# Two transformer blocks in one program: the residual x stored by features instead of by tokens

## Chip, cores, metric

One core of one Trainium2 chip. The number compared is the device time of one execution in microseconds (us); a lower one is better. Three executions of the kernel before took 1293.08, 1286.48 and 1292.35 us, a median of 1292.35 us.

## The reference

Input is x with 256 tokens of 1024 features, two memories of 256 tokens (`mem`, `mem_2`) and all weights, everything in fp32. Two blocks follow one another. Cut to the lines that matter here:

```python
# block 1, layer 0 (retention) and layer 1 (differential attention)
memn = rms_norm(mem, mem_norm_w)
for layer in range(2):
    u = rms_norm(x, attn_norm_w[layer]) @ w_in[layer]
    o_main = ...            # retention, or differential attention with q, k normed per head
    o_mem = memory_attention(rms_norm(qc), ...memn @ w_mem_kv[layer]...)
    x = x + concat([o_main, o_mem]) @ w_out[layer]
    gu = rms_norm(x, ffn_norm_w[layer]) @ w_gate_up[layer]
    x = x + (silu(gu[..., :FFN_DIM]) * gu[..., FFN_DIM:]) @ w_down[layer]
# block 2
proj = rmsnorm(x, norm_mix_g) @ w_in_2
merged = sigmoid(gate_a) * y_gdn + sigmoid(gate_b) * y_gla     # two chunked recurrences
x = x + merged @ w_out_2
m = rmsnorm(mem_2, norm_mem_g)                                  # keys and values of cross attention
x = x + cross_attention(rmsnorm(x, norm_xattn_g), m) @ xattn_wo
x = x + square(relu(rmsnorm(x, norm_mlp_g) @ mlp_w1)) @ mlp_w2
return rmsnorm(x, norm_final_g)
```

`rms_norm(x, w)` is x divided by the root of the mean of its squares over the 1024 features (plus 1e-6), times w.

## The kernel before, in words

**Products in three parts.** Every weight product splits both operands into a high and a low part in fp32r and adds hi*hi, hi*lo and lo*hi in PSUM. Weights stream through `unit` (L261): one unit is two row blocks of 128 by up to 512 columns. Its steps are a load by SP's queue into `raw` (3 buffers), a cast to `hi` by ACT (L277) and a subtraction to `lo` by DVE (L185; every 8th unit by POOL). `hi` and `lo` have 4 buffers each. There are three ways to multiply with a unit:

- `proj` (L290): the activations are stationary, the weights move 512 columns. 12 matmuls a unit, two accumulators, and the result has a token on each partition.
- `proj_T` (L311): the weights are stationary, the activations move 256 columns.
- `proj_T2` (L338): the weights are stationary. High and low part of the activations lie side by side (`both`), so one matmul moves 512 columns for hi times both parts, and one of 256 adds lo times hi. 16 matmuls a unit, four accumulators of [128, 2, 256] whose two halves must be added afterwards, and the result has a feature on each partition.

**The residual.** x is two tiles of 128 tokens by 1024 features (`setup`, L367), loaded in `setup_rest` (L385). Each product that is added to it (`w_out`, `w_down`, `w_out_2`, `xattn_wo`, `mlp_w2`) goes through `out_proj` (L510): `proj` for the first 512 columns, an addition into x (`add_x`, L502), `proj` for the other 512, and another. The next layer wants x by features: `x_T2` (L636) transposes it with 4 PE transposes for each pair of features and splits the result into `H` tiles. `_Lazy` makes these splits when they are first asked for, so those of the first half of x are asked for while the second half's product runs (L514).

**Norms.** The products of a layer start with unnormalized x times the norm's gain. The factor of each token comes from `stats` (L245): four ACT squares with an accumulator, POOL's `rsqrt` (L200), and it is applied later. For the two memories `mem_stats` (L400) loads their rows for the same purpose, while `scaled_T` (L391) loads them transposed, in four loads of 512 KB into tiles of tag 'V', and splits them into `Z` tiles. The mixer multiplies x by the factor before it transposes (L774).

**Buffers and order.** `BUFS` (L144) sets how many buffers a tag has:

```python
BUFS = {'T': 14, 'G': 6, 'L': 22, 'H': 4, 'Z': 12, 'B': 4, 'V': 3}
```

A tile gets the buffer that was given out longest ago, and waits until that is read for the last time. 'V' serves the loads of `scaled_T` and the scratch of squares. The order of instructions on each engine is made by the scheduler of the tile framework from its own estimates when the program is built; on the chip each engine then works its list in order. `later` (L202) additionally holds an instruction behind the `lo` of a unit some units on.

**The start of the diff layer** (L645) comes right after ffn0's down product. PE runs two products of four units (`proj` at L648 and L752), then `scores(0, ...)` transposes the normalized result of the first, the `Z<-acc,tiny` tiles of L677. Between, DVE and ACT split the transposed mem_2 (L650), and `head_rms` (L406) computes the factors: square, reduction, POOL's `rsqrt` on 128x8.

## Time and profile before

| what | value |
| --- | --- |
| median of 3 runs | 1292.35 us (1286.48 to 1293.08) |
| the profiled execution | 1287.81 us, its span 1286.1 us, so 1.7 us lie around the span |
| PE busy | 1250.5 us, 97% of the span |
| DVE, ACT, POOL busy | 828.1, 678.8, 180.9 us (64%, 53%, 14%) |
| DMA | 215.72 MB, 168 GB/s on average |

The profiled execution is 4.5 us below the median. PE is busy nearly throughout, so two things move the time: what PE has to do, and the 36 us (1286.1 less 1250.5) in which it waits. Other engines matter where PE waits for them.

### The profile page before, as it was taken

How to read it: one execution, taken by the hardware profiler on the slowest of the kernel's cores; microseconds unless marked ns; L12 is line 12 of the kernel's file. 1: busy time of each engine (PE TensorE's matmuls, PEld its weight loads, DVE VectorE, ACT ScalarE, POOL GpSimd, SP SyncE). 2: the span in 40 equal slices, each digit the busy share in tenths (PEclk: the TensorE clock that was granted, in tenths of full speed). 3: DMA queues.
4: the chain of work that ended last, by engine and by line, in shares of the span. 5: the costliest groups of instructions: out<-in, count | busy, mean ns of one | idle time of the engine just before them, and what ended most of it. 6: DMA issues, size and time to landing. Idle time of an engine off the chain costs nothing.

```text
span 1286.1 us, 19034 instructions
## 1 busy us (share of the span) xinstructions
PE 1250.5 (97%) x7160; PEld 1071.6 (83%) x7160; DVE 828.1 (64%) x1299; ACT 678.8 (53%) x1088; POOL 180.9 (14%) x115
## 2 busy tenths in 40 slices
PE   8999999999999999999998999999999999999997
PEld 8787888888778888888878998867788897888886
DVE  6576677755876667674467787486635665788542
ACT  5655656545664565554467573343344444565442
POOL 0122110010420110100101021221111000001011
PEclk9999999999999999999999999999999999999999
DMA  8826566656644256665653545224365552565653
GB/s 297 279 87 203 176 196 185 196 195 192 187 131 148 83 164 201 192 190 189 195 176 115 181 121 170 84 70 142 112 194 175 172 177 86 166 207 178 201 190 107
DMA packets 147005, 215.72 MB, mean 168 GB/s; under 512 B 15456, under 2 KB 71904, under 8 KB 146912
## 3 DMA queue, kind: packets, MB, share of 16 engines
q1 hardware_dynamic: 146336, 213.27, 53.3%
q8 instruction: 56, 0.92, 0.3%
q10 hardware_dynamic: 432, 0.70, 0.2%
q0 software_dynamic: 144, 0.52, 0.1%
q14 instruction: 37, 0.30, 0.1%
HBM read 213.02 MB, written 1.44 MB: 167 GB/s over the span
## 4 chain that ended last, share of the span: by engine, by line
PE 84%; DVE 6%; DMA 3%; ACT 3%; issue 2%; POOL 1%; SPq 1%; POOLq 0%; ACTq 0%; DVEq 0%
PE acc L207 74%; PE ps L207 7%; PE ps L210 2%; DVE lo L185 2%; ACT hi L277 1%; DVE T L185 1%; DMA raw<-in_w_in_dram 1%; POOL tiny L200 1%; DVE L L185 1%; ACT T L195 1%; SPq L1053 0%; DMA constants<-in_small_dram 0%; DVE B L185 0%; DMA B<-in_mem_dram 0%; SPq L1029 0%
## 5 line engine op out<-in xcount | busy, mean ns | idle before, releaser
L277 ACT CAST hi<-raw 128x1024 fp32r<-128x1024 f32 (+1 forms) x393 | 407.1, 1039 | 413.3 <-PE acc L207 326.7
L185 DVE TENSOR_TENSOR lo<-raw,hi 128x1024 fp32r<-128x1024 f32 (+1 forms) x341 | 412.5, 1214 | 316.5 <-ACT hi L277 312.3
L207 PE MATMUL acc<-H,hi 128*128 128x512 f32 (+1 forms) x1696 | 470.5, 347 | 1.8 <-ACT hi L277 1.7
L207 PE MATMUL acc<-H,lo 128*128 128x256 f32 x1328 | 372.2, 281 | 0.0
L207 PEld LDWEIGHTS acc<-H,hi 128*128 128x128 f32 x1696 | 296.3, 190 | 43.7 <-ACT hi L277 2.5
L207 PEld LDWEIGHTS acc<-H,lo 128*128 128x128 f32 x1328 | 252.4, 190 | 1.8 <-issue 0.8
L185 POOL TENSOR_TENSOR lo<-raw,hi 128x1024 fp32r<-128x1024 f32 (+1 forms) x52 | 124.2, 2389 | 796.2 <-ACT hi L277 618.8
L207 PE MATMUL acc<-hi,H 128*128 128x512 f32 (+1 forms) x672 | 212.4, 392 | 1.2 <-ACT H L195 0.6
L207 PE MATMUL acc<-hi,Z 128*128 128x512 f32 x544 | 171.4, 391 | 0.0
L207 PE MATMUL acc<-hi,L 128*128 128x512 f32 x512 | 160.2, 390 | 0.0
L207 PEld LDWEIGHTS acc<-hi,H 128*128 128x128 f32 x672 | 125.3, 189 | 27.9 <-issue 1.8
L207 PE MATMUL acc<-lo,H 128*128 128x512 f32 (+1 forms) x336 | 131.6, 392 | 0.8 <-DVE lo L185 0.8
L207 PEld LDWEIGHTS acc<-hi,Z 128*128 128x128 f32 x544 | 102.1, 188 | 20.9
L207 PEld LDWEIGHTS acc<-hi,L 128*128 128x128 f32 x512 | 96.1, 188 | 19.8
L207 PE MATMUL acc<-lo,Z 128*128 128x512 f32 x272 | 106.0, 390 | 0.0
L207 PE MATMUL acc<-lo,L 128*128 128x512 f32 x256 | 99.7, 390 | 0.0
L207 PEld LDWEIGHTS acc<-lo,H 128*128 128x128 f32 x336 | 63.6, 189 | 14.6 <-DVE lo L185 1.7
L200 POOL TENSOR_TENSOR tiny<-tiny,constants 128x2 f32<-128x2 f32 (+4 forms) x41 | 41.4, 1012 | 238.6 <-DVE tiny L189 190.2
L207 PEld LDWEIGHTS acc<-lo,Z 128*128 128x128 f32 x272 | 51.1, 188 | 10.2
L207 PEld LDWEIGHTS acc<-lo,L 128*128 128x128 f32 x256 | 48.1, 188 | 9.8
L357 ACT COPY T<-acc 128x256 f32<-128x256 f32 x120 | 43.8, 369 | 12.8 <-PE acc L207 9.3
L185 DVE TENSOR_TENSOR T<-acc,T 128x256 f32<-128x256 f32 x120 | 44.9, 416 | 2.1 <-ACT T L357 2.1
(218 smaller groups left out, 1109.3 us busy)
## 6 DMA issues: line engine op xcount, KB each, us to landing
raw<-in_w_in_dram SPq DMA_DIRECT2D x91, 512.0 KB, 3.7
raw<-in_w_gate_up_dram SPq DMA_DIRECT2D x176, 256.0 KB, 3.4
raw<-in_mlp_w_dram SPq DMA_DIRECT2D x64, 512.0 KB, 4.3
raw<-in_w_down_dram SPq DMA_DIRECT2D x44, 512.0 KB, 4.5
raw<-in_w_out_dram SPq DMA_DIRECT2D x24, 512.0 KB, 4.3
raw<-in_w_in_dram SPq DMA_DIRECT2D x42, 256.0 KB, 3.9
raw<-in_w_mem_kv_dram SPq DMA_DIRECT2D x8, 512.0 KB, 3.9
raw<-in_xattn_wk_dram SPq DMA_DIRECT2D x8, 512.0 KB, 3.8
```

The costliest lines, as they stand in the source:

```text
L185: return (eng or self.nc.vector).tensor_tensor(out=out, in0=a, in1=b, op=op)
L195: self.nc.scalar.activation(out, in_, f, scale=scale, bias=bias, **k)
L200: self.nc.gpsimd.tensor_tensor(out=out, in0=in_, in1=self.c('mhalf')[:, :n], op=ALU.pow)
L207: self.nc.tensor.matmul(out, lhsT, rhs, start=start, stop=stop, skip_group_check=True)
L210: self.nc.tensor.transpose(out, in_, self.ident[:in_.shape[0], :in_.shape[0]])
L277: nc.scalar.copy(hi[:, k, :W], raw[:, k, :W])
L357: self.nc.scalar.copy(out[:, a, :], accs[a][:, 1, :])
```

## The change

x lives in four tiles of [128, 2, 256] by features. They are loaded from the transposed input directly (`first_T`), and neither x nor the memories are loaded by rows any more: six loads of 512 KB are gone. The four products `w_out` (both layers), `w_down` (both), `w_out_2` and `xattn_wo`, 76 units in all, go through `proj_T2`, and `add_x` adds both halves of each accumulator into x, in ffn after a product with the row R of factors. `x_T2` splits x without a transpose. `stats` squares x on ACT, adds the squares on DVE into a 'G' tile, and gets the mean with two matmuls with a column of 1/1024. For the memories the squares are taken of the transposed tiles in `scaled_T`, so that loads, squares and the sum of the products in `add_x` share the three 'V' buffers. `mlp_w2` keeps `proj`; `rows` transposes x back for it with 16 transposes. The constants' first 16 columns are loaded ahead of the others. `split` makes one tile a feature block, and 'H' has 8 buffers.

```diff
-    BUFS = {'T': 14, 'G': 6, 'L': 22, 'H': 4, 'Z': 12, 'B': 4, 'V': 3}
+    BUFS = {'T': 14, 'G': 6, 'L': 22, 'H': 8, 'Z': 12, 'B': 4, 'V': 3}
...
+    def squares(self, sums, x):
+        if not sums:
+            sums.append(self.t('G', F32, (P, 2, S)))
+            self.act(sums[0], x, AF.Square)
+        else:
+            j = self.t('V', F32, (P, 2, S))
+            self.act(j, x, AF.Square)
+            self.tt(sums[0], sums[0], j, ALU.add)
...
+    def stats(self, sums=None):
+        if sums is None:
+            sums = []
+            for p in range(4):
+                self.squares(sums, self.x[p])
+        ps = self.psum(tag='sm')
+        v = sums[0][:, 0, :]
+        self.tt(v, v, sums[0][:, 1, :], ALU.add)
+        for t in range(2):
+            self.mm(ps[:, t:t + 1], v[:, t * P:(t + 1) * P], self.mean)
         ms = self.tiny(2)
...
+        self.ts(ms, ps[:, :2], EPS, ALU.add)
...
     def setup(self):
...
-        self.x = [self.cp.tile([P, D], F32, name=f"x{t}") for t in range(2)]
+        self.x = [self.cp.tile([P, 2, S], F32, name=f"x{p}") for p in range(4)]
...
-        nc.scalar.dma_start(out=self.const[:, :w1], in_=a['small'][:, :w1])
+        nc.scalar.dma_start(out=self.const[:, :w0], in_=a['small'][:, :w0])
+        nc.sync.dma_start(out=self.x[0], in_=a['xT'][:, 0:2, :])
+        nc.scalar.dma_start(out=self.const[:, w0:w1], in_=a['small'][:, w0:w1])
...
-    def scaled_T(self, src, gname, tag):
+    def scaled_T(self, src, gname, tag, sums):
         def pair(p):
             raw = self.t('V', F32, (P, 2, S))
             self.nc.sync.dma_start(out=raw, in_=src[:, 2 * p:2 * p + 2, :])
-            return self.split(raw, tag, [self.col(gname, 2 * p + a) for a in range(2)])
+            out = self.split(raw, tag, [self.col(gname, 2 * p + a) for a in range(2)])
+            self.squares(sums, raw)
+            return out
...
-    def mem_stats(self, ap):
-        m = [self.t('B', F32, (P, D)) for _ in range(2)]
-        for t in range(2):
-            self.nc.sync.dma_start(out=m[t], in_=ap[t * P:(t + 1) * P, :])
-        return self.stats(m)
...
     def add_x(self, accs, c, scale=None):
...
+        for f, acc in enumerate(accs):
+            x = self.x[2 * c + f // 2][:, f % 2, :]
+            if scale is None or isinstance(scale, float):
+                for h in range(2):
+                    if scale is None:
+                        self.tt(x, acc[:, h, :], x, ALU.add)
+                    else:
+                        self.stt(x, acc[:, h, :], scale, x, ALU.mult, ALU.add)
             else:
...
+                e = self.t('V')[:, :S]
+                self.nc.scalar.copy(e, acc[:, 1, :])
+                self.tt(e, acc[:, 0, :], e, ALU.add)
+                self.tt(e, e, scale)
+                self.tt(x, x, e, ALU.add)
...
-        self.add_x(self.proj(hT, w, [(0, 512)], order), 0, scale)
+        self.add_x(self.proj_T2(hT, w, [(0, 512)], order, None, only), 0, scale)
...
+    def x_T2(self, gname, off=0, R=None):
+        def pair(p):
+            cols = [self.col(gname, off + 2 * p + a) for a in range(2)]
+            if R is None:
+                return self.split(self.x[p], 'H', cols)
+            n = self.t('V', F32, (P, 2, S))
+            for a in range(2):
+                self.stt(n[:, a, :], self.x[p][:, a, :], cols[a], R)
+            return self.split(n, 'H')
...
     def diff_layer(self):
...
-        ms, r = self.stats(self.x)
-        mT2 = self.mT2 = self.scaled_T(self.a['mem_2T'], 'mem2', 'Z')
+        ms, r = self.stats()
+        self.m2sums = []
+        mT2 = self.mT2 = self.scaled_T(self.a['mem_2T'], 'mem2', 'Z', self.m2sums)
         mT2[7]
```

**What moves on the engines.** The lists that follow are the instructions of one engine in their order in the program; numbers after a name tell tiles apart.

DVE at the start of the diff layer, before: `Z_3208` and `Z_3216` are parts of mem_2, `lo_3297` and `lo_3316` the last two units of the second product, `Z_3242` is the first normalized tile, for which PE's transposes wait.

```order
312 L192 SCALAR_TENSOR_TENSOR Z_3208<-V_3205,constants,Z_3207 128x256 x2
313 L192 SCALAR_TENSOR_TENSOR Z_3216<-V_3213,constants,Z_3215 128x256 x2
314 L411 TENSOR_REDUCE tiny_3237<-V_3235 128x8
315 L189 TENSOR_SCALAR tiny_3237<-tiny_3237,tiny_3221 128x8
316 L185 TENSOR_TENSOR lo_3297<-raw_3293,hi_3296 128x1024
317 L411 TENSOR_REDUCE tiny_3246<-V_3244 128x8
318 L185 TENSOR_TENSOR lo_3316<-raw_3312,hi_3315 128x1024
319 L185 TENSOR_TENSOR Z_3242<-acc_3077,tiny_3240 128x512
320 L189 TENSOR_SCALAR tiny_3246<-tiny_3246,tiny_3221 128x8
321 L185 TENSOR_TENSOR lo_3441<-raw_3437,hi_3440 128x1024
```

DVE there, after: `V_3397` and `V_3408` are the last two loads of mem_2, `V_3405` and `V_3416` their squares, `lo_3514` the last unit of the second product, `lo_3639` to `lo_3677` units of the third, `Z_3440` the first normalized tile.

```order
381 L192 SCALAR_TENSOR_TENSOR Z_3402<-V_3397,constants,Z_3402 128x256
382 L185 TENSOR_TENSOR G_3384<-G_3384,V_3405 128x512
383 L185 TENSOR_TENSOR lo_3639<-raw_3635,hi_3638 128x1024
384 L185 TENSOR_TENSOR lo_3658<-raw_3654,hi_3657 128x1024
385 L192 SCALAR_TENSOR_TENSOR Z_3410<-V_3408,constants,Z_3410 128x256
386 L192 SCALAR_TENSOR_TENSOR Z_3413<-V_3408,constants,Z_3413 128x256
387 L185 TENSOR_TENSOR G_3384<-G_3384,V_3416 128x512
388 L432 TENSOR_REDUCE tiny_3435<-V_3433 128x8
389 L185 TENSOR_TENSOR lo_3677<-raw_3673,hi_3676 128x1024
390 L189 TENSOR_SCALAR tiny_3435<-tiny_3435,tiny_3419 128x8
391 L185 TENSOR_TENSOR G_3384<-G_3384 128x256
392 L185 TENSOR_TENSOR Z_3440<-acc_3267,tiny_3438 128x512
```

Between the last `lo` of the second product and the first normalized tile there stood nothing; now there stand the splits of the last two loads of mem_2, the additions of their squares and three units.

SP's queue there, before: the loads of mem_2 among those of the weights, with what each waits for.

```order
189 L395 DMA V_3189<-in_mem_2T_dram 128x512 [waits Activation_49]
190 L395 DMA V_3197<-in_mem_2T_dram 128x512 [waits Activation_49]
191 L395 DMA V_3205<-in_mem_2T_dram 128x512 [waits DMAHW0_49,Activation_49]
192 L271 DMA raw_3293<-in_w_in_dram 128x2x256 [waits DMAHW1_49,DVE_49]
193 L271 DMA raw_3293<-in_w_in_dram 128x2x256 [waits DMAHW2_49]
194 L271 DMA raw_3312<-in_w_in_dram 128x2x256 [waits DMAHW3_49,DVE_49]
195 L395 DMA V_3213<-in_mem_2T_dram 128x512 [waits DMAHW6_49,DMAHW4_49,DVE_49]
```

SP's queue there, after:

```order
184 L281 DMA raw_3491<-in_w_in_dram 128x2x256 [waits DMAHW4_49,DMAHW5_49,DVE_49,Activation_49]
185 L412 DMA V_3376<-in_mem_2T_dram 128x512 [waits DVE_49,Activation_49]
186 L281 DMA raw_3491<-in_w_in_dram 128x2x256
187 L412 DMA V_3386<-in_mem_2T_dram 128x512 [waits DVE_49]
188 L281 DMA raw_3510<-in_w_in_dram 128x2x256 [waits DMAHW1_49,DMAHW6_49,DMAHW0_49,Pool_49]
189 L281 DMA raw_3510<-in_w_in_dram 128x2x256 [waits DMAHW7_49]
190 L281 DMA raw_3635<-in_w_in_dram 128x2x256 x2
191 L412 DMA V_3397<-in_mem_2T_dram 128x512 [waits DMAHW2_49,DMAHW3_49,DVE_49,Activation_49]
192 L281 DMA raw_3654<-in_w_in_dram 128x2x256 [waits DMAHW4_49,DVE_49]
193 L281 DMA raw_3654<-in_w_in_dram 128x2x256
194 L412 DMA V_3408<-in_mem_2T_dram 128x512 [waits DMAHW5_49,DVE_49]
```

Three of the four loads stood together and waited for ACT; now each of the four waits for DVE, and loads of weights stand behind each.

DVE between the two halves of layer 0's `w_out`, before (`lo_1314` and `lo_1332` are the second half's first two units):

```order
130 L189 TENSOR_SCALAR L_1193<-ps_1188,qkw 128x512
131 L185 TENSOR_TENSOR lo_1314<-raw_1311,hi_1313 128x1024
132 L185 TENSOR_TENSOR lo_1332<-raw_1329,hi_1331 128x1024
133 L185 TENSOR_TENSOR x_75<-acc_1195,x_75 128x512
134 L185 TENSOR_TENSOR x_76<-acc_1196,x_76 128x512
135 L185 TENSOR_TENSOR lo_1375<-raw_1371,hi_1374 128x1024
```

DVE there, after (`lo_1313` and `lo_1347` are the second half's first two units, `acc_1206` to `acc_1209` the first half's result):

```order
147 L192 SCALAR_TENSOR_TENSOR H_1332<-x_75,constants,H_1332 128x256
148 L185 TENSOR_TENSOR lo_1313<-raw_1310,hi_1312 128x1024
149 L185 TENSOR_TENSOR T_1179<-acc_1106,tiny_1195 128x256
150 L185 TENSOR_TENSOR x_76<-acc_1208,x_76 128x256
151 L185 TENSOR_TENSOR x_76<-acc_1209,x_76 128x256
152 L189 TENSOR_SCALAR L_1204<-ps_1199,qkw 128x512
153 L185 TENSOR_TENSOR x_76<-acc_1208,x_76 128x256
154 L185 TENSOR_TENSOR x_76<-acc_1209,x_76 128x256
155 L192 SCALAR_TENSOR_TENSOR H_1335<-x_75,constants,H_1335 128x256
156 L192 SCALAR_TENSOR_TENSOR H_1338<-x_76,constants,H_1338 128x256
157 L192 SCALAR_TENSOR_TENSOR H_1341<-x_76,constants,H_1341 128x256
158 L185 TENSOR_TENSOR lo_1347<-raw_1344,hi_1346 128x1024
```

Ahead of the second unit's `lo` there stood no addition into x; now the additions and splits of the first half do.

## Rows read from the trace of the kernel before

**Rows 1.** The page: span, and busy time of each engine with its share and instructions.

```profile
span 1286.1 us, 19034 instructions
...
PE 1250.5 (97%) x7160; PEld 1071.6 (83%) x7160; DVE 828.1 (64%) x1299; ACT 678.8 (53%) x1088; POOL 180.9 (14%) x115
```

**Rows 2.** Timeline of PE in ffn0's up projection: a `proj_T2` stretch. Columns: start us, us.

```profile
198.73 0.39 PE L207 MATMUL acc<-H,hi 128*128 128x512 f32 x1
...
204.27 0.39 PE L207 MATMUL acc<-H,hi 128*128 128x512 f32 x1
```

**Rows 3.** Timeline of PE in ffn0's down projection: a `proj` stretch.

```profile
299.83 0.62 PE L207 MATMUL acc<-hi,Z 128*128 128x512 f32 x2
...
302.55 0.62 PE L207 MATMUL acc<-hi,Z 128*128 128x512 f32 x2
```

**Rows 4.** Groups of PE by shape, then the timeline around one group of eight transposes of x.

```profile
L210 PE MATMUL ps<-constants,x 128*128 128x128 f32 x80 | 10.4, 272 | 0.0
...
L210 PE MATMUL ps<-constants,B 128*128 128x128 f32 x16 | 2.2, 279 | 0.7 <-DVE B L189 0.7
...
138.21 1.03 PE L210 MATMUL ps<-constants,x 128*128 128x128 f32 x8
139.00 0.48 PE L207 MATMUL acc<-H,hi 128*128 128x512 f32 x1
139.32 0.28 PE L207 MATMUL acc<-H,lo 128*128 128x256 f32 x1
```

**Rows 5.** Timeline of PE in the retention layer: 32 small matmuls.

```profile
77.55 3.68 PE L207 MATMUL ps<-L,T 128*128 128x64 f32 x32
```

**Rows 6.** Timeline of ACT and PE at the start; the landing of tile V there (us).

```profile
5.62 0.91 ACT L195 ACTIVATE H<-V,constants 128x256 fp32r<-128x256 f32 x2 [2.88 <-DMA constants<-in_small_dram]
...
7.08 1.22 PE L207 MATMUL acc<-H,hi 128*128 128x256 f32 x4 [1.75 <-ACT hi L277]
...
DMA to landing us min/median/max: 4.5/4.9/6.4
```

**Rows 7.** Busy time by stretch, a column per engine: PE first; then clock, DMA share, GB/s.

```profile
40.00:50.00 10.00, 8.91 (x39) 6.77 (x38) 5.55 (x10) 7.74 (x13) 2.39 (x1) 1.00 0.90 302
```

**Rows 8.** Groups by shape (busy us, mean ns | idle us before): DVE, ACT, POOL.

```profile
L185 DVE TENSOR_TENSOR lo<-raw,hi 128x1024 fp32r<-128x1024 f32 x332 | 406.5, 1228 | 312.7 <-ACT hi L277 308.6 <-PE acc L207 3.6
L185 DVE TENSOR_TENSOR T<-acc,T 128x256 f32<-128x256 f32 x120 | 44.9, 416 | 2.1 <-ACT T L357 2.1
L192 DVE SCALAR_TENSOR_TENSOR H<-ps,constants,H 128x256 fp32r<-128x256 f32 x56 | 24.4, 478 | 3.3 <-ACT H L195 2.9
...
L195 ACT ACTIVATE V<-x 128x512 f32<-128x512 f32 x32 | 19.9, 622 | 12.5 <-DVE x L192 11.0 <-DVE lo L185 0.8 <-DMA x<-in_x_dram 0.8
...
L200 POOL TENSOR_TENSOR tiny<-tiny,constants 128x8 f32<-128x8 f32 x6 | 11.8, 1973 | 16.4 <-DVE tiny L189 16.4
```

**Rows 9.** Timeline of DVE at the start of the diff layer.

```profile
316.76 1.40 DVE L192 SCALAR_TENSOR_TENSOR x<-acc,tiny,x 128x512 f32<-128x512 f32 x2
...
328.75 1.93 DVE L192 SCALAR_TENSOR_TENSOR Z<-V,constants,Z 128x256 fp32r<-128x256 f32 x2 [1.66 <-ACT Z L195]
...
334.36 0.69 DVE L185 TENSOR_TENSOR Z<-acc,tiny 128x512 f32<-128x512 f32 x1
```

**Rows 10.** Timeline of PE there.

```profile
340.15 1.03 PE L210 MATMUL ps<-constants,Z 128*128 128x128 f32 x8
...
343.00 1.57 PE L207 MATMUL ps<-T,T 64*128 64x128 f32 x12 [0.45 <-ACT T L690]
...
353.04 0.59 PE L210 MATMUL ps<-constants,T 128*128 128x128 f32 x2 [1.86 <-DVE T L192]
```

**Rows 11.** Timeline of SP's queue there, and the landing of tile V (us).

```profile
318.95 1.55 SPq L395 DMA_DIRECT2D V<-in_mem_2T_dram  x3
...
323.96 0.34 SPq L395 DMA_DIRECT2D V<-in_mem_2T_dram  x1
...
DMA to landing us min/median/max: 3.5/4.4/4.6
```

More of the change, by code (lines that the diff above doesn't have):

```diff
@@ L328, in proj_T, with acc2, proj_T2 @@
         return accs
-    def acc2(self):
+    def acc2(self, only=None):
         self.n += 1
         self.n2 += 1
-        if self.n2 % 3:
+        if only or self.n2 % 3:
             return self.pa.tile([P, 2, S], F32, tag="acc", name=f"acc{self.n}")
         return self.ps.tile([P, 2, S], F32, tag="pg", name=f"acc{self.n}", bufs=2)
-    def proj_T2(self, hT, w, cols):
+    def proj_T2(self, hT, w, cols, order=None, meanwhile=None, only=None):
         W = sum(b for _, b in cols)
-        accs = [self.acc2() for _ in range(W // P)]
+        accs = [self.acc2(only) for _ in range(W // P)]
         n = len(hT)
-        for k0 in range(0, n, 2):
-            hT[k0]
-            hi, lo = self.unit(w, k0, 2, cols)
+        order = order or list(range(n))
+        for i in range(0, n, 2):
+            hT[order[i]]
+            if i == 2 and meanwhile:
+                meanwhile()
+            hi, lo = self.unit(w, order[i], 2, cols)
             for f in range(W // P):
@@ L1393, in run @@
         else:
-            for t in range(2):
-                self.nc.sync.dma_start(out=self.a['out'][0, t * P:(t + 1) * P, :], in_=self.x[t])
+            for t, x in enumerate(self.rows()):
+                self.nc.sync.dma_start(out=self.a['out'][0, t * P:(t + 1) * P, :], in_=x)
 @with_exitstack
```

155 lines of the change are left out of this document (75 added, 80 removed).

## The prediction

> **What bounds the kernel now.** I read the totals first: PE is busy 1250.5 us of a span of 1286.1, so only 35.6 us are waits of PE; DVE has 64% and ACT 53% [rows 1]. Work taken from DVE or ACT is therefore worth nothing by itself, work on PE counts in full, and every step that makes PE wait counts in full too. Next I read PE's rhythm in the two kinds of stretches whose exchange is the change: the start of equal matmuls in `proj_T2` [rows 2] and in `proj` [rows 3], and the price of eight transposes between two products [rows 4]. Then I looked for the places at which PE waits or nearly waits and which the change touches: the start [rows 6], the stretch full of DMA behind it [rows 7], and the start of the diff layer, where four views belong together: DVE's list [rows 9], PE's [rows 10], SP's queue and the landing of its loads [rows 11], and the durations of single operations [rows 8]. The sums are made against the profiled execution's 1287.8 us; the median of the runs, 1292.35 us, stands 4.5 above it, and I carry the difference over to the median.
>
> **PE's work: -2.7 us.** Transposes: 96 are removed (80 with x as input, 16 with the mixer's B) and 16 of `rows` come, so 80 fewer. Eight took 138.21 to 139.00, 0.79 us, and the next matmul was followed after 0.32 us in place of the 0.23 that others take, so 0.88 us for eight, 0.11 each [rows 4]. 80 x 0.11 = -8.8 us; without the delay behind them it would be -7.9. Products: 16 pairs of `proj_T2` took 198.73 to 204.27, so a unit of 8 pairs takes 2.77 us [rows 2]; a unit of `proj` takes 299.83 to 302.55, 2.72 us [rows 3]. 76 units x 0.05 = +3.8 us. The means: 18 matmuls of one column and two more for a row. The nearest row is 32 small ones in 3.68 us, 0.115 each [rows 5], so 20 x 0.115 = +2.3; they may fall where PE waits anyway, so 0 is the other end. I take the full price, since PE hardly waits. Sum -8.8 + 3.8 + 2.3 = -2.7.
>
> The Trainium skill ("TensorE: Matmul & The Clock Gate", section Back-to-back issue gap) gives an isolated gap of N/2.4 + 2.5 ns, 215.8 ns for 512 columns and 109.2 for 256. By it a unit of 16 matmuls would take 2.60 us and one of 12 would take 2.59, and 76 units would cost 0.8 us in place of 3.8; the rows disagree with both absolute numbers, and the trace decides.
>
> **The start: -1.** ACT's first split waited 2.88 us for the constants, at 5.62, and PE's first real matmul came at 7.08 [rows 6]. Now 16 columns come first. But that split also needs the load of x, which takes 4.5 to 6.4 us to land, 4.9 in the middle, so the load becomes the limit almost at once. A gain between 0 and 2.5; I take 1.
>
> **Fewer loads: -0.3.** Six loads of 512 KB, 3 MB, go, most of them in a stretch where DMA is at 0.90. There PE loses 10.00 - 8.91 = 1.1 us in ten [rows 7], which is the most that can come back there; part of that wait belongs to steps of ACT. I take 0.3.
>
> **Half boundary of layer 0's `w_out`: +1.** The additions into x now stand ahead of the `lo` of the second half's second unit. Behind the end of the first half DVE has about two additions of 128x256 at 0.42, one 128x512 operation at about 0.7, three splits at 0.48 and the `lo` of 1.23 [rows 8], together 4.2 us; PE has the first unit, 2.77, and a pair of the next, 0.35 [rows 2]. So PE waits 1.1 us. If ACT's casts come late it is 2; if the additions begin inside the last unit, as their accumulators end one after the other, 0. I take 1. At the other boundaries the same additions stand behind two prepared units, 5.4 us, against 12 operations of 0.42 and a split, 5.5: I put 0.5 on all of these together (0 to 2).
>
> **The start of the diff layer: +8.** This is the term that decides. Call T the end of ffn0's down product, 316.7 in the trace [rows 9]. Before, the four loads of mem_2 left SP at T+2 (three) and T+7 [rows 11], DVE had the last split of them at T+14 and the first normalized tile at T+18.4, done before PE came to the transposes at T+23.4 [rows 9, 10]. So PE waited there for nothing, and soon after for 0.45 and 1.86 us [rows 10].
>
> After, PE arrives earlier: 8 units of 2.72, T+21.8. But the three 'V' buffers now hold scratch of the additions, three squares of x, four loads and three squares of mem_2. The chain, with durations of rows 8 and pitches slightly below them: 12 additions and products of x (0.33 to 0.42 each), two splits, the `lo` that stands ahead, and the first addition of squares bring DVE to about T+8; only then is a buffer free and the first load leaves. The second leaves after the next addition, T+10, and lands 4.4 us later [rows 11], at T+14.4. Its two casts (1.0) and square (0.62), then DVE's splits, a `lo` and the addition of the square: T+17. That addition frees the buffer of the fourth load, which lands at T+21.5. Casts and square, DVE's two splits, the addition: T+24. Then, in DVE's list, stand a reduction (0.67), a `lo` (1.23), a small scaling (0.2), POOL's `rsqrt` of 128x8 (1.97) and at last the first normalized tile (0.7): about T+28.5. PE waits 6.6 us. Then it has 13 matmuls (3 us) until the second tile, for which DVE and POOL need another 4.3: 1.3 us. Of the later waits I assume 1.4 and 1.6 in place of the former 0.45 and 1.86. 6.6 + 1.3 + 3.0 - 2.3 = +8.6; I take 8. Lower bound +3: the two loads that follow one another land in 3.5 us each and DVE works at its pitch, 3.6 us less in all, with the later waits as before. Upper bound +12: splits that collide on the memory take 1.5 us like the one of two in 1.93 us at 328.75 [rows 9], and SP's queue holds the loads of weights behind each blocked load of mem_2, so that the third product's units are late as well.
>
> That the buffers are what PE would wait for is also what the Trainium skill says of such gaps ("Perfetto Trace Analysis", section Optimization Strategy): consistent bubbles on the engine that should be full can mean that no memory is free for the next tile. No row here shows this for 'V', since in the kernel before the same three buffers were enough.
>
> Work that costs nothing: 173 more DVE instructions, mostly 128x256 halves of what was 128x512, and 67 on ACT lie beside PE, as long as DVE keeps a third of its time free [rows 1]; without that cover they would be about 173 x 0.42 = 73 us of DVE. The mixer's product with the row replaces the scaling that PE waited for before (0.7 us, [rows 4], last field of the B group), so it is put at nothing.
>
> **Sum.** -2.7 - 1 - 0.3 + 1 + 0.5 + 8 = +5.5 us: 1293.3 against the profiled 1287.8, and 1297.9 against the median 1292.35, +0.43%. A measurement of this kernel can tell about 0.5% (6.4 us) from no change, so the forecast is no change that can be told, on the slow side.
>
> **Rivals.**
> - *The 'V' chain costs its upper price (slower).* At the start of the diff layer, if a load of mem_2 leaves SP more than some 1 us later than I laid out, everything behind it moves: +12 instead of +8, and the boundaries 1 more. 1292.35 + 5.5 + 5 = 1303. For it speaks that each load waits for an addition in DVE's list that itself waits for ACT, against it that SP's loads of weights have three buffers of lead. It decides from +6.4 in all, hence already 1 us beyond my sum.
> - *The chain keeps up (faster).* If DVE's additions run early and loads land in 3.5 us, PE waits no more than before there: -2.7 - 2.5 - 1.1 + 0 + 0 = -6.3, 1286. For it speaks that PE's work does shrink; against it that the Z tile stands behind the last load of mem_2 in DVE's list, whatever the loads do.
> - *The pitch of the page's rule.* If the exchange of products cost 0.8 us in place of 3.8, the time would be 3 less, 1294.9, still no change. The rows at both kinds of stretches speak against it: 5 in 100.
> - *The change does less than it says.* Transposes come back for `mlp_w2`: counted. I see no other.
>
> **Chances.** The forecast with its near bounds, and the rule's case, 0.46; slower by over 0.5% 0.42; faster by over 0.5% 0.12. The range takes in the faster rival's 1286 and the upper price's 1303 and, on either side, what medians of three runs scatter here (the three shown span 6.6, so some 3): 1283 to 1306.
>
> **What would show it.** Right: 16 transposes of x in PE's groups, no accumulators of `proj` in the four products; PE's busy time about 3 us less; the first matmul at about 6; in the diff layer a wait of PE of about 6 us ahead of the transposes of Z, released by DVE's Z, with loads of mem_2 spread over some 12 us. Wrong: no such wait, or PE's busy time that grows; or a wait of several us at the start of another layer (the mixer, ffn1), which would mean that I looked at the wrong place.

## The result, and the profile after

| | before | after |
|---|---|---|
| median of four runs | 1290.07 us (1286.48 to 1293.08) | 1326.73 us (1322.11 to 1331.07) |
| the profiled execution | 1287.8 us | 1325.7 us |
| its span / its mean granted clock | 1286.1 us / 0.996 | 1324.0 us / 0.981 |

The ratio is 1.0285, with an interval of 1.0237 to 1.0333: slower, and outside the range of the prediction (1283 to 1306), which had called 1297.9 and no change that can be told. A second, later set of runs gave 1327.25 against 1296.89 (after_again, below).

The totals of the changed kernel's page, to be laid beside [rows 1]:

```profile
span 1324.0 us, 19807 instructions
...
PE 1268.6 (96%) x7424; PEld 1090.9 (82%) x7424; DVE 877.5 (66%) x1472; ACT 687.9 (52%) x1118; POOL 181.3 (14%) x115
```

Two differences stand in these two lines. PE's waits, span less busy time, went from 35.6 to 55.4 us: **+19.8**. PE's busy time went from 1250.5 to 1268.6: **+18.1**, although the work was to shrink by 2.7. Most of this second gap is the clock. These are the sums over all stretches at a granted clock of 0.50, ten after and two before, without the one behind the last product (us, then each engine's busy time in them, PE's first):

```profile
sum 44.37, PE 39.15 PEld 33.09 DVE 29.76 ACT 15.48 POOL 5.14; mean PE 3.91 PEld 3.31 DVE 2.98 ACT 1.55 POOL 0.51
```

```profile
sum 6.83, PE 6.83 PEld 5.56 DVE 5.79 ACT 3.05 POOL 0.00; mean PE 3.42 PEld 2.78 DVE 2.90 ACT 1.53 POOL 0.00
```

A pair of products takes 0.64 us there in place of 0.347 (rows of waits_in_before below), so 0.46 of PE's busy time in them is lost: 17.9 us after and 3.1 before, some **15 us** more. That is an estimate. 19.8 + 15 makes 35 of the 37.9 us by which the span grew; the other 3 are what is left for PE's work at full clock, where -2.7 had been forecast.

The ledger by stages, from PE's timeline of both kernels (ends, us after the span's start, and what each stage added):

| up to the end of | before | after | added |
|---|---|---|---|
| the first `mem_kv` | 63.96 | 71.45 | +7.5 |
| ffn0's up product | 256.44 | 273.16 | +9.2 |
| ffn0's down product | 317.22 | 334.18 | +0.2 |
| the diff layer's head, to the first product of `xattn_k` | 387.00 | 413.99 | +10.0 |
| ffn1's up product | 582.33 | 612.17 | +2.9 |
| ffn1's down product | 642.22 | 673.18 | +1.1 |
| the mixer's head, to its gated product | 691.28 | 725.55 | +3.3 |
| the linear layer (`gla`) | 986.42 | 1019.88 | -0.8 |
| the `mlp`'s up product | 1191.29 | 1229.31 | +4.6 |
| the `mlp`'s down product | 1278.34 | 1316.37 | 0.0 |

The one stage on which the forecast rested has its +10. The two first stages have 16.7 together, and those behind it 11. The longer waits of PE that the change brought, by its timeline (the bracket holds the wait and the writer of what it waited for):

```profile
29.87 2.76 PE L207 MATMUL ps<-T,T 64*128 64x256 f32 x16 [1.42 <-DVE tiny L189]
...
51.66 0.58 PE L207 MATMUL ps<-mean,G 128*128 128x1 f32 x4 [2.59 <-DVE G L185]
...
145.87 0.47 PE L207 MATMUL acc<-H,hi 128*128 128x512 f32 x1 [3.15 <-DVE x L185]
...
159.75 0.49 PE L207 MATMUL ps<-T,constants 128*128 128x128 f32 x2 [0.70 <-DVE T L189]
162.03 0.80 PE L207 MATMUL ps<-T,constants 128*128 128x128 f32 x2 [1.79 <-DVE T L189]
...
346.37 0.60 PE L207 MATMUL ps<-mean,G 128*128 128x1 f32 x4 [1.28 <-DVE G L185]
...
364.91 0.69 PE L210 MATMUL ps<-constants,Z 128*128 128x128 f32 x2 [6.92 <-DVE Z L185]
...
462.73 1.54 PE L210 MATMUL ps<-constants,T 128*128 128x128 f32 x6 [2.02 <-DVE T L185]
...
701.65 0.31 PE L210 MATMUL ps<-constants,T 32*128 32x32 f32 x2 [1.79 <-DVE T L895]
```

The one of 6.92 us was predicted. At 701.65 stand the mixer's gates, at 462.73 the diff layer's later heads, where three shorter waits make it 4.4 us for 2.6 before. The others are of two kinds: small matmuls (the mean's, the row's) or the small operations behind them, for which PE stands ahead of products which are ready, and, at 145.87, four accumulators of `w_out[0]` that DVE's additions into x still hold.

And the clock behind such waits: busy time in stretches of 4 us of the changed kernel (PE's stands first, then PEld, DVE, ACT, POOL; then the granted clock, DMA share, GB/s).

```profile
160.00:164.00 4.00, 2.21 (x9) 1.82 (x9) 3.77 (x6) 0.46 (x2) 1.90 (x1) 0.69 0.62 186
164.00:168.00 4.00, 4.00 (x23) 3.52 (x22) 1.78 (x3) 2.70 (x3) 0.00 (x0) 0.88 0.21 70
...
360.00:364.00 4.00, 0.00 (x0) 0.00 (x0) 2.63 (x5) 2.75 (x5) 1.62 (x1) 0.86 0.77 217
364.00:368.00 4.00, 3.09 (x9) 2.51 (x10) 3.15 (x5) 0.00 (x0) 1.33 (x2) 0.50 0.48 130
368.00:372.00 4.00, 4.00 (x19) 3.25 (x17) 2.37 (x6) 0.51 (x1) 2.12 (x3) 0.78 0.35 120
...
464.00:468.00 4.00, 3.09 (x12) 2.53 (x11) 2.52 (x7) 1.82 (x5) 0.26 (x1) 0.50 0.00 0
...
720.00:724.00 4.00, 4.00 (x15) 3.42 (x14) 3.28 (x5) 1.42 (x4) 0.00 (x0) 0.50 0.04 14
```

0.50 is the lower of the clock's two levels, 1.2 GHz, for a whole stretch. Before, two places fell at all (352 to 360 us to 0.89 and 0.69, 684 to 692 to 0.77 and 0.80); now ten do, and six of them (near 32, 52, 161, 363, 462 and 704 us) lie at or behind a wait that the change brought or made longer. The other four (8, 718, 957 and 1104) lie behind waits that the kernel before has as well.

### The profile page after: what moved, and what is told of

The parts are those of the page before. It is cut to its first block, busy times and chain, and to the rows that moved or that the text cites. A ratio compares the mean times of both kernels' runs of the same rounds, so it can differ in the third digit from the quotient of the medians.

```text
span 1324.0 us, 19807 instructions
## 1 busy us (share of the span) xinstructions
PE 1268.6 (96%) x7424; PEld 1090.9 (82%) x7424; DVE 877.5 (66%) x1472; ACT 687.9 (52%) x1118; POOL 181.3 (14%) x115
## 4 chain that ended last, share of the span: by engine, by line
PE 81%; DVE 7%; issue 4%; DMA 3%; ACT 3%; POOL 2%; SPq 1%; POOLq 0%; ACTq 0%; DVEq 0%
PE acc L207 72%; PE ps L207 7%; PE ps L210 2%; DVE lo L185 2%; DMA raw<-in_w_in_dram 1%; ACT hi L287 1%; POOL tiny L200 1%; DVE T L185 1%; ACT T L195 1%; DVE L L185 1%; DMA V<-in_mem_2T_dram 0%; SPq L1097 0%; DVE G L185 0%; DMA V<-in_memT_dram 0%; DVE tiny L189 0%
## 5 line engine op out<-in xcount | busy, mean ns | idle before, releaser
L207 PE MATMUL acc<-L,hi 128*128 128x512 f32 x352 | 124.4, 398 | 0.2
L207 PE MATMUL acc<-Z,hi 128*128 128x512 f32 (+1 forms) x384 | 114.4, 361 | 0.0
L207 PE MATMUL acc<-L,lo 128*128 128x256 f32 x352 | 97.7, 281 | 0.3 <-DVE lo L185 0.3
L207 PE MATMUL acc<-hi,Z 128*128 128x512 f32 x288 | 90.2, 390 | 0.0
L207 PE MATMUL acc<-Z,lo 128*128 128x256 f32 x320 | 89.6, 281 | 0.0
L207 PEld LDWEIGHTS acc<-L,hi 128*128 128x128 f32 x352 | 66.4, 190 | 15.6 <-ACT L L195 0.4
L207 PEld LDWEIGHTS acc<-Z,hi 128*128 128x128 f32 x384 | 67.9, 189 | 12.3 <-issue 1.0
L207 PEld LDWEIGHTS acc<-L,lo 128*128 128x128 f32 x352 | 66.8, 190 | 1.4 <-DVE lo L185 0.9
L207 PEld LDWEIGHTS acc<-hi,Z 128*128 128x128 f32 x288 | 54.0, 188 | 11.1
L207 PEld LDWEIGHTS acc<-Z,lo 128*128 128x128 f32 x320 | 60.4, 189 | 0.8 <-issue 0.7
```

The source lines that it names most:

```text
L207: self.nc.tensor.matmul(out, lhsT, rhs, start=start, stop=stop, skip_group_check=True)
```

## The experiments

Theory A, formed on this: the change puts short waits into PE's list at several layer heads, and the clock falls behind them, so that a wait costs more than its length. Theory V: the squares and the scratch of additions in 'V' make the waits, with the held accumulators as a second source. The rivals: only waits count, and the clock is chance; or the work itself grew. For each ratio the kernel before ran beside on the same chip; there it took 1294 to 1298 us. Each edit also lets the scheduler order every engine's list anew, so a run differs by more than its edit; its waits are read besides its time.

### What a wait costs

**waits_in_before.** The kernel before, with five waits put into a stretch where PE never waits (ffn0's up product): accumulators that stay in use until POOL has run a chain of 1 to 8 operations. The four small matmuls at each place write values that the products overwrite.

```diff
...
-            accs = self.proj_T2(hT, wg, [(c * 256, 256), (FFN + c * 256, 256)])
+            gate, steps = None, {2: 1, 4: 2, 6: 3, 8: 5, 10: 8}.get(c, 0) if l == 0 else 0
+            if steps:
+                gate = self.tiny(2)
+                self.ts(gate, accs[3][:, 1, S - 2:], 0.0, ALU.mult, 1.0, ALU.add)
+                for _ in range(steps):
+                    g, gate = gate, self.tiny(2)
+                    self.rsqrt(gate, g)
+            accs = self.proj_T2(hT, wg, [(c * 256, 256), (FFN + c * 256, 256)], gate)
```

> The kernel before, with five waits of PE put into ffn0's up product and nothing else: ahead of every second group of columns four tiny matmuls wait for a chain of 1, 2, 3, 5 and 8 POOL operations of about 0.7 us that starts from the group's last accumulator. The waits should be about 1.0, 1.8, 2.5, 4.0 and 6.3 us, 15.6 in all, with PE's work unchanged. Theory A (in the changed kernel a wait costs PE its own length and then again a stretch at a granted clock of 0.5): stretches at 0.5 follow the longer waits, as in the changed kernel (some 4 us, costing 1.7 to 2 us each), and the time grows by 15.6 plus 3 times 1.8, about 21 us. Rival B (the lower clock of the changed kernel comes from its other products, not from waits): the clock stays as before, and the time grows by about 16 us.

Measured: 1352.31 us, ratio 1.0419 (1.0398 to 1.0440). The sum of PE's waits there, by the view of waits:

```profile
PE acc L207 <- POOL tiny L200: 33.3, 5, 9.9
```

and the first of the five and what followed, by stretches:

```profile
159.00:163.00 4.00, 0.84 (x4) 0.84 (x5) 3.13 (x6) 1.58 (x4) 1.20 (x1) 0.87 0.70 214
163.00:167.00 4.00, 4.00 (x14) 3.54 (x15) 0.00 (x0) 0.00 (x0) 0.00 (x0) 0.50 0.14 45
167.00:171.00 4.00, 4.00 (x20) 3.49 (x19) 0.80 (x1) 1.05 (x1) 0.00 (x0) 0.78 0.00 0
```

Two pairs of products there, which start 0.64 us apart:

```profile
164.68 0.63 PE L207 MATMUL acc<-H,hi 128*128 128x512 f32 x1
...
165.32 0.63 PE L207 MATMUL acc<-H,hi 128*128 128x512 f32 x1
```

The waits were longer than planned, 33.3 us for 15.6, and so was the time: +56 for the +21 of theory A. The up product from the row on took 162.8 us (147.75 to 310.54) in place of 109.2: +53.6, of which 33.3 are waits and 20.3 more busy time. The small matmuls are 5 x 0.91 = 4.6 of these (0.91 at full clock, in the next run). The other 15.7 us, 3.1 for each wait, are what products and small matmuls took longer at half clock. These waits, of 4.8 to 9.9 us, are longer than all but one that the change brought.

**waits_filled.** The same, with 20 to 41 throwaway products of 512 columns ahead of each of the five places, on data at hand.

```diff
+            for _ in range(fill):
+                self.mm(accs[0], hT[0][0][:, :P], hT[0].both)
```

> The kernel before with the same five waits as in the run waits_in_before, but ahead of each stand 20, 19, 22, 33 and 41 matmuls of 512 columns whose result is thrown away, 0.227 us each, so that PE works while the chain of POOL runs (30.6 us of filler against 33.3 us of wait). The real products resume at nearly the same times. Theory A (the granted clock falls because PE stood idle): the clock stays near 1.00 in ffn0, PE's waits there are under 5 us in all, and the time is that of waits_in_before less what the clock cost, 4 us for each of five waits: 1330 to 1336 us beside 1352. Rival B (the clock fell for another reason, such as the tiny fp32 matmuls at the end of each wait): the stretches at 0.5 stay, and the time is within 3 us of 1352 or above.

Measured: 1341.73 us, ratio 1.0324 (1.0280 to 1.0368), so 10.6 us less, with the intervals apart, but not the 16 to 22 less of the expectation. The same stretches:

```profile
159.00:163.00 4.00, 4.00 (x22) 3.40 (x21) 2.54 (x5) 2.55 (x5) 0.00 (x0) 1.00 0.80 260
163.00:167.00 4.00, 3.17 (x18) 2.39 (x16) 3.16 (x6) 1.78 (x4) 1.21 (x1) 1.00 0.66 200
167.00:171.00 4.00, 4.00 (x25) 3.52 (x25) 0.13 (x1) 0.68 (x1) 0.00 (x0) 1.00 0.17 59
```

PE has 30.6 us more work (135 products at 0.227) and is done sooner: that the clock falls where PE stands, and that this costs time of its own, is shown here. A dip behind the second place stayed (0.60 in 198 to 202, behind a rest of the wait of 1.06 us).

### Which part of the change makes the waits

**after_again.** The changed kernel itself once more, run last, since the parts below were measured at other times than the first pair, on three chips.

> The changed kernel once more, for the comparisons: in the other runs the kernel before took 1294 to 1298 us, some 5 to 8 us more than beside the changed kernel's first runs (1290.07). If both kernels shift alike, the ratio comes out in 1.0237 to 1.0333 again and the ratios of the parts can be compared with 1.0285. Rival: the changed kernel does not shift, 1326.7 against some 1296, ratio about 1.0235; then accs_shared (1.0198), and to a part scratch_b and after_filled, gained only half of what their ratios say.

Measured: 1327.25 us (1320.39 to 1329.44) against 1296.89; ratio 1.0216 (1.0172 to 1.0260). The rival on this point: the changed kernel's time is the same, and the kernel before is 7 us slower there. So a part is judged by its time as well, and a ratio whose interval overlaps 1.0172 to 1.0260 shows no gain. The Z wait was there again (7.10 us), with seven of the ten low places; the other waits moved by up to 2.4 us (4.94 for 2.59 ahead of the memory's mean).

**scratch_b.** The scratch of squares and additions in buffers 'B' in place of 'V', up to the diff layer.

```diff
-            j = self.t('V', F32, (P, 2, S))
+            j = self.t(self.scr, F32, (P, 2, S))
...
-                e = self.t('V')[:, :S]
+                e = self.t(self.scr)[:, :S]
```

> The changed kernel, where the scratch of squares and of the additions into x uses tag B (idle in the first block) in place of V, so that the loads of the transposed memories have the three V buffers nearly to themselves. Theory (buffers of V hold up the loads of mem_2): the wait of 6.92 us ahead of the transposes of Z in the diff layer goes, with the stretch at a lower clock behind it, and the wait of 2.59 us for the sum of mem's squares shrinks: 9 to 12 us less than the changed kernel, 1315 to 1318 us. Rival (DVE has too much to do there, whatever the buffers): the wait shrinks by less than 2 us, and the time is 1324 to 1327.

Measured: 1318.97 us, ratio 1.0189 (1.0151 to 1.0226), 8 us under the changed kernel with overlapping intervals. The Z wait is gone, and another came a step further on in PE's list:

```profile
364.43 2.08 PE L208 MATMUL ps<-T,T 64*128 64x128 f32 x10 [3.21 <-ACT T L740]
```

So the buffers are what held Z back, and behind them stands ACT's next tile, for which PE waits 3.21 us in place of 6.92. The wait ahead of the memory's mean did not shrink as expected but stayed at 2.72.

**accs_shared.** Both `w_out` without `only=True`: accumulators from both PSUM pools, as in the up products.

```diff
-        self.xT = self.out_proj(oT + omT, ..., gname='ffn', only=True)
+        self.xT = self.out_proj(oT + omT, ..., gname='ffn')
```

> The changed kernel, where both w_out products take every third accumulator from the other PSUM pool, as the up products do, in place of all four from one pool. Theory (with four accumulators of the pool held by the product until DVE has added them into x, the next layer's product can't start): the wait of 3.15 us at ffn0's start goes or falls below 1, 3 to 5 us less, 1322 to 1324. Rival (DVE is late with the split of x anyway): the wait only moves to the H tiles, and the time stays within 1 us of the changed kernel's 1326.7.

Measured: 1322.97 us, ratio 1.0198 (1.0173 to 1.0223): 4 us less than the changed kernel, as theory said, but not told from no gain. The wait of 3.15 us at `w_out[0]` is gone, that of the row matmuls behind it is 2.39 in one piece.

**mem_rows.** The memories' mean squares from loads by rows, as before; x stays by features.

```diff
-        sums = []
-        self.memT = self.scaled_T(self.a['memT'], 'mem', 'Z', sums)
...
-        ms, r = self.stats(sums)
+        ms, r = self.mem_stats(self.a['mem'])
```

> The changed kernel, where the mean squares of the two memories are taken of their rows as in the kernel before (four loads of 512 KB more, ACT squares with an accumulator, no sums on DVE and no matmul for them). Theory (the squares of the memories in the V tiles make the chain of loads long, and their mean's matmul stands in PE's list): the wait of 2.59 us goes, the wait of 6.92 us shrinks to 2 or 3, as the fourth load no longer waits for the sum of a square; 6 to 9 us less, 1318 to 1321, less the cost of the loads in a stretch where DMA is busy (up to 1 us). Rival (x's own squares and additions in V hold up the loads): the wait of 6.92 stays above 5, and the gain is 3 us.

Measured: 1315.58 us, ratio 1.0152 (1.0136 to 1.0167), under the changed kernel's on both pairs, and 11 to 12 us less where 6 to 9 had been expected. The wait of 2.59 us is gone. Of the Z wait 1.30 us are left, and the clock is 1.00 behind it:

```profile
357.31 0.99 PE L210 MATMUL ps<-constants,Z 128*128 128x128 f32 x7 [1.30 <-DVE Z L185]
```

Something else went with them. In the changed kernel the row's chain ends in two scalings by DVE, which took 2.57 us beside a subtraction (`lo`) by POOL, and PE waited 0.70 + 1.79 us for them. Here POOL's subtraction came only after they had begun; they took 0.48 us, and PE did not wait for the row:

```profile
155.41 0.48 DVE L189 TENSOR_SCALAR T<-constants,tiny 128x128 f32<-128x128 f32 x2 [0.81 <-POOL tiny L200]
155.75 2.40 POOL L185 TENSOR_TENSOR lo<-raw,hi 128x1024 fp32r<-128x1024 f32 x1 [0.37 <-ACT hi L287]
155.99 0.61 PE L207 MATMUL ps<-T,constants 128*128 128x128 f32 x4
```

So a part of the gain is not the memories'.

**mem_cols.** The opposite: the kernel before with the memories' part of the change alone.

```diff
+            if sums is not None:
+                self.squares(sums, raw)
...
-        ms, r = self.mem_stats(self.a['mem'])
+        ms, r = self.col_stats(sums)
```

> The kernel before with one part of the change alone: the mean squares of the two memories by products with a column, from squares summed by DVE, no loads by rows; x stays by rows. Theory V (the squares of the memory in V hold back its next loads, DVE's first normalized tile Z comes late, and the clock falls behind the wait): a wait of PE of 2 to 7 us ahead of the first transposes from Z, one of 2 to 3 us ahead of the memory's mean matmuls, 9 to 17 us in all, ratio 1.007 to 1.013. Rival (the chain is only long because the additions and squares of x stand ahead of it): no wait of over 2 us ahead of Z, ratio 1.000 to 1.004.

Measured: 1301.19 us against 1294.33, ratio 1.0054 (1.0018 to 1.0089). Both waits came:

```profile
46.13 0.58 PE L207 MATMUL ps<-mean,G 128*128 128x1 f32 x4 [2.46 <-DVE G L185]
...
347.38 1.76 PE L210 MATMUL ps<-constants,Z 128*128 128x128 f32 x7 [3.10 <-DVE Z L185]
```

The part costs 7 us by itself, with waits as theory V said and a sum below its 9 to 17; by the time alone the rival's 1.000 to 1.004 would not be excluded, by the waits it is. Taken out of the changed kernel it gives 11 to 12. What makes the other 4 to 5 us was not measured: with the additions and squares of x ahead in the same buffers the Z wait is 6.92 and not 3.10, and the row's wait went in mem_rows by POOL's timing.

### What is left

**rows_shared.** mem_rows and accs_shared together.

> The changed kernel with two of the former edits together: mean squares of the memories from rows (mem_rows) and w_out's accumulators from both PSUM pools (accs_shared). Theory (these are separate waits at separate places): the gains add, the waits of 2.59, 3.15 and 6.92 us are all gone or under 1.5: about 13 parts in 1000 for the first and up to 8 for the second below the changed kernel's 1.0285, so a ratio of 1.007 to 1.012. Rival (the waits move on to the next late step, the row of factors in ffn0): the ratio stays at 1.015, with a wait of about 2 us for the row in ffn0's first group.

Measured: 1312.06 us, ratio 1.0123 (1.0084 to 1.0162), not told from mem_rows. The waits of 2.59, 3.15 and 6.92 us are gone or under 1.5, as theory said, and the row's is back, as the rival said, with POOL's subtraction beside the scalings again:

```profile
148.58 2.34 POOL L185 TENSOR_TENSOR lo<-raw,hi 128x1024 fp32r<-128x1024 f32 x1
148.65 2.55 DVE L189 TENSOR_SCALAR T<-constants,tiny 128x128 f32<-128x128 f32 x2 [0.81 <-POOL tiny L200]
151.06 1.22 PE L207 MATMUL ps<-T,constants 128*128 128x128 f32 x4 [2.38 <-DVE T L189]
```

**rows_held.** That, with the mean's matmuls (diff layer) and the row's (both ffn) moved behind later products in PE's list.

```diff
-            self.mm(ps[:, t:t + 1], v[:, t * P:(t + 1) * P], self.mean)
+            i = self.mm(ps[:, t:t + 1], v[:, t * P:(t + 1) * P], self.mean)
+            if hold:
+                self.later(i, hold)
```

> rows_shared, and besides the matmuls of the mean at the diff layer's start and those of the row of factors in both ffn are held behind later units, so that they stand some 35 matmuls later in PE's list. Theory (a small matmul that waits for a chain of ACT, DVE and POOL holds up PE's whole list): the waits of 1.28 us for the sum of squares and of up to 2.4 us for the row go, 2 to 4 us less than rows_shared and one stretch at a low clock fewer: a ratio of 1.004 to 1.009. Rival (PE would wait for the accumulators or the normalized tiles anyway): no difference from rows_shared beyond 1 us.

Measured: 1316.54 us, ratio 1.0125 (1.0081 to 1.0170). The row's wait of 2.38 is gone, and these stand in its and the mean's place:

```profile
152.74 0.77 PE L207 MATMUL acc<-H,hi 128*128 128x512 f32 x1 [1.99 <-DVE T L185]
...
355.98 0.44 PE L210 MATMUL ps<-constants,Z 128*128 128x128 f32 x2 [1.74 <-DVE Z L185]
358.56 1.54 PE L210 MATMUL ps<-constants,Z 128*128 128x128 f32 x6 [1.21 <-DVE tiny L189]
```

The waits sum to 4.9 us, and so they do in rows_shared (2.38 + 1.28 + 1.30): a later place in PE's list alone gains nothing, as the rival said. At 152.74 PE waits for accumulators that DVE's additions free, and these stand in DVE's list behind the row's scalings, which took 2.58 us beside POOL's subtraction here too, where mem_rows has 0.48:

```profile
149.68 2.58 DVE L189 TENSOR_SCALAR T<-constants,tiny 128x128 f32<-128x128 f32 x2 [0.81 <-POOL tiny L200]
152.18 1.40 DVE L185 TENSOR_TENSOR T<-acc,T 128x256 f32<-128x256 f32 x4
```

**rows_scratch.** rows_shared with the scratch of scratch_b.

> rows_shared (ratio 1.0123) with the scratch of squares and additions outside V as in scratch_b. Theory V: with the memory's means from rows the V buffers hardly hold anything back any more, only the waits ahead of Z and T of 1.3 us each in the diff layer can go with their clock, 1 to 4 us, ratio 1.009 to 1.0115. Rival (the scratch in V costs of its own, wherever it stands): the 12 us that scratch_b gained come again, ratio 1.003 to 1.005.

Measured: 1306.07 us, ratio 1.0089 (1.0052 to 1.0127), the best of the versions with x by features, but still 12 us above the kernel before. It lies at the lower end of theory V's span, and the rival's 1.003 to 1.005 is just outside the interval; from rows_shared it is not told apart.

### Filling the waits of the changed kernel

Throwaway products ahead of the waits, in place of shorter chains:

```diff
+    def fill(self, ps, n):
+        x = self.h0
+        for _ in range(n):
+            self.mm(..., x[0][:, :P], x.both)
```

**after_filled.** 10 ahead of the memory's mean, 9 ahead of ffn0's row, 26 ahead of the first transposes from Z.

> The changed kernel with throwaway matmuls of 512 columns (0.227 us each in the trace) ahead of three of its waits: 10 ahead of the memory's mean matmuls (wait 2.59 us), 9 ahead of ffn layer 0's row matmuls (waits 0.70 and 1.79 us), 26 ahead of the differential layer's first transposes from Z (wait 6.92 us). They compute nothing that is used; the waits are then filled and not shortened. Theory A (the fall of the granted clock behind a wait costs time of its own): the stretches at a granted clock of 0.5 and 0.6 behind these three places go, the sum of the waits falls by some 10 us, PE's busy time grows by no more than 10 us less 5 to 6 us, and the time falls by 5 to 6 us, to a ratio of 1.023 to 1.024 to the kernel before. Rival (the clock's low stretches are chance, or come from elsewhere): the ratio stays at 1.0285, and the same stretches are low.

Measured: 1330.83 us, ratio 1.0268 (1.0236 to 1.0299): no gain. The expectation failed. The waits ahead of the mean and the row kept 1.68 and 1.70 us, with the clock at 1.00 behind them, and ahead of Z this happened:

```profile
358.68 6.05 PE L207 MATMUL ps<-H 128*128 128x512 f32 x26
365.92 0.44 PE L216 MATMUL ps<-constants,Z 128*128 128x128 f32 x2 [1.19 <-DVE Z L185]
...
370.23 1.12 PE L216 MATMUL ps<-constants,Z 128*128 128x128 f32 x4 [3.40 <-DVE Z L185]
```

PE comes through the products between the first and the second Z faster, and stands 3.40 us ahead of the second, behind which the clock falls. In the changed kernel the half clock had used up just that time; the second Z stands there without a wait:

```profile
370.63 0.82 PE L210 MATMUL ps<-constants,Z 128*128 128x128 f32 x6
```

Where one late chain feeds several steps, the low clock costs nothing until the chain has caught up. Of the fillers' 10.2 us, 7.0 appear in PE's busy time (1275.6), and the waits stay at 53.7.

**rows_filled.** rows_shared with 9 ahead of ffn0's row and 7 ahead of the mixer's gates.

> rows_shared (memory means from rows as before, four accumulators shared; ratio 1.0123) with 9 throwaway matmuls of 512 columns ahead of ffn layer 0's row matmuls (wait 2.38 us there) and 7 ahead of the mixer gates' transposes (waits 1.84 and 3.35 us). Theory A: the low clock behind these two places goes, some 4 us less, ratio about 1.009. Rival (the fillers only lie in front of the work): ratio 1.0123 or more.

Measured: 1309.22 us, ratio 1.0091 (1.0058 to 1.0125). The mean is the one that theory A gave, the intervals of both overlap: unclear. In the trace the clock is 1.00 behind the row's wait, now 1.26 us, and ffn0's up product from the row on took 111.5 in place of 113.2 us. Behind the gates, whose wait is now 0.84 us, the clock fell all the same (0.50 in 692 to 694).

## Why the prediction was wrong

- **The wait ahead of Z: right.** Forecast 6.6 us, measured 6.92; the loads of mem_2 were laid out at T+8, T+10 and, for the last, some T+17:

```profile
341.19 0.34 SPq L412 DMA_DIRECT2D V<-in_mem_2T_dram  x1
345.08 0.34 SPq L412 DMA_DIRECT2D V<-in_mem_2T_dram  x1
347.66 0.35 SPq L412 DMA_DIRECT2D V<-in_mem_2T_dram  x1
351.39 0.34 SPq L412 DMA_DIRECT2D V<-in_mem_2T_dram  x1
```

  With T at about 333.7 these are T+7.5, 11.4, 14.0 and 17.7. The first normalized tile was done at T+31 and not T+28.5, and PE too came 2.5 us later than said: that the two errors cancel is luck. An operation that no term held lies on both ways: a `lo` of DVE took 3.42 us at 341.04, beside POOL's, in place of 1.22, and the additions for which PE waited 1.28 us stand behind it. The stage's +10.0 stands against +8. scratch_b shows the buffers as the cause.
- **PE's work, -2.7: right where it can be read alone, wrong in sum.** ffn0's down product has no wait: 22 units at 0.05 more, less eight transposes at 0.88, makes +0.2; it took 61.02 for 60.78. By the estimate above the work grew by some 3 us. Some 2.4 of the miss are the means, priced with the row's at 2.3: 18 matmuls show as 36 instructions, 4.7 us busy. Some stretches ran at a slower pitch (last section).
- **The start and the loads: wrong by a little.** The first product began at 6.85 for 7.08, and its whole run ended at 26.62 for 26.05: nothing gained. In the stage full of DMA the 0.3 us did not show, for the stage grew by 7.5.
- **"The means ... I take the full price" and "I put 0.5 on all of these together": the step that failed first.** I counted the mean's and the row's matmuls by what PE does in them, and not by what PE waits for in front of them. Each ends a chain of additions and squares, the row's also of POOL's root and DVE's scalings, that PE now has to sit out, in order, with ready products behind: 2.59 + 0.70 + 1.79 + 1.28 us by the rows above. mem_cols brought such a wait back alone; rows_held shows that moving it in PE's list alone gains nothing. Most of the row's 2.49 us goes back to POOL's subtraction beside the scalings, 2.57 us for 0.48, as the trace of mem_rows shows; the forecast had no term for that.
- **"Half boundary of layer 0's w_out: +1": too high, and the boundary behind it too low.** Inside `w_out[0]` PE waited 0.30 us for the `lo` (at 134.21). The 3.15 us stand at its end, ahead of ffn0's first product, one of the boundaries for which 0.5 was put on all together, from two units being prepared. What PE missed there were accumulators and no unit. DVE's list shows the additions that free them behind a weight's `lo`:

```profile
144.17 1.23 DVE L185 TENSOR_TENSOR lo<-raw,hi 128x1024 fp32r<-128x1024 f32 x1 [3.26 <-ACT hi L287]
145.31 2.07 DVE L185 TENSOR_TENSOR x<-acc,x 128x256 f32<-128x256 f32 x6
...
159.41 2.57 DVE L189 TENSOR_SCALAR T<-constants,tiny 128x128 f32<-128x128 f32 x2 [0.81 <-POOL tiny L200]
```

  The `lo` waited 3.26 us for its cast, which waited for a load, and the additions waited behind it. accs_shared took this wait away.
- **The mixer's row, "put at nothing": mis-sized.** The mixer's head grew by 3.3 us; its gates wait 1.79 us for DVE, and the clock is low behind them.
- **No term for the clock: the largest miss, some 15 us.** I priced a wait at its length. The trace of before had the sign of it: behind the 1.86 us wait at 353.04 [rows 10] its clock was 0.89 and then 0.69. waits_in_before and waits_filled show the price there, 3.1 us for a wait of 5 to 10 us. In the changed kernel it is estimated only in sum, by busy time and clock; after_filled did not get it back. The Trainium skill ("TensorE: Matmul & The Clock Gate", section HAM oscillation — how this bites in real kernels) has this as a rule: a wait that recurs makes the clock fall at each recurrence, and the time spent throttled costs half of itself. The trace comes near that half: a pair of products in 0.64 us behind the first of the five waits, for 0.347 at full clock, loses 0.46. Not only recurring waits cost the clock here: it also fell behind the single ones of 1.42 and 2.59 us.
- **The sum.** 8 + 1 + 0.5 of waits against +19.8, a clock at 0 against some +15, and work at -2.7 against some +3. The slower rival (1303) had the place right and the size wrong, because it too held one mechanism at one place. The sign that the prediction named for itself, busy time that grows, came about; what made it grow was for the most part not work. So did the other one, waits at the start of other layers (ffn0, the mixer).

What stays open: of the 12 us that rows_scratch is still above the kernel before, the row's wait of 2.38 us (POOL's subtraction again) and its clock are seen, and several low stretches elsewhere; how they divide was not measured. No run kept POOL's subtractions away on purpose. And which of two similar waits is followed by a low clock I can't say from these runs.

## What to carry to other kernels

Where PE is busy 97% of the span, a matmul is priced by the chain that ends in it, not by its columns: ask of every small matmul that a change adds what stands behind it in PE's list and when its operand comes. A new wait of PE costs its length and often a stretch of products at half clock behind it, unless the same chain would have made PE wait there anyway. What lies beside a step of the chain on another engine belongs to its price. A saving of loads and transposes has to pay for the buffers and for DVE's place in line that it takes at a layer's head.

## What the runs showed of the hardware

- Two levels of pitch at full clock: a pair of `proj_T2` came every 0.347 us in most stretches, and every 0.353 in others, for tens of us at a time, without a wait and at a granted clock of 1.00. In the `mlp`'s up product, after and before, eight pairs apart:

```profile
1180.03 0.40 PE L207 MATMUL acc<-H,hi 128*128 128x512 f32 x1
...
1182.85 0.40 PE L207 MATMUL acc<-H,hi 128*128 128x512 f32 x1
```

```profile
1149.88 0.39 PE L207 MATMUL acc<-H,hi 128*128 128x512 f32 x1
...
1152.65 0.39 PE L207 MATMUL acc<-H,hi 128*128 128x512 f32 x1
```

  2.82 us and 2.77. Over a product of 256 pairs that makes some 1.5 us; no run tells what sets it.
- The kernel before scatters with its clock: eleven executions beside after_again ran from 1288.01 us at a mean clock of 0.996 to 1304.71 at 0.984.
- A DVE operation on SBUF tiles that began while POOL ran a `lo` mostly ended only about when POOL's did. Two scalings of 128x128 took 2.57 us at 159.41 beside POOL's `lo` of 2.40 from 159.50, and 0.48 in mem_rows; two splits of 128x256 took 2.75 at 47.70 beside POOL's from 47.39, and 0.87 elsewhere; a `lo` took 3.42 at 341.04 beside POOL's from 340.93, and 1.22 elsewhere. Of the DVE operations that began during POOL's 52 subtractions in the changed kernel, 24 of the 29 on SBUF tiles alone were held so, and none of the 29 that read an accumulator or a PSUM tile. All three examples lie on chains that PE waited for; the memory's mean was waited for without the slow splits too (2.72 us in scratch_b). The Trainium skill ("GPSIMD Engine Reference", section 8. Key points) says that POOL shares its SBUF interfaces with VectorE, with contention for DVE instructions in a 2-port perf mode or with two SBUF inputs; the trace agrees on the contention, and does not show the mode of the scalings.
